# Four of six modulation parts as running sums on VectorE, placed between the delta rule's first pair of heads and the retention

## The chip, the cores and the metric

The kernel runs on 1 core of one Trainium2 chip. The metric is the device time of one execution in microseconds (us). The whole program is one launch: a first transformer block (a retention and a gated delta rule side by side, then a mixture of experts) and a second one.

## What is computed

Only the modulation matters here. A conditioning vector goes through silu and a 1024 by 6144 matrix, a bias is added, and the 6144 results are cut into six vectors of 1024: shift, scale and gate of the mixer, shift, scale and gate of the feed-forward part. The first two of the six are also wanted for a second vector, that of the context.

```python
def _modulation(cvec, w, b, n):
    m = jax.nn.silu(cvec) @ w[:, : n * D_MODEL] + b[: n * D_MODEL]
    return jnp.split(m, n, axis=-1)
...
        sh1, sc1, g1, sh2, sc2, g2 = [m[:, None, :] for m in _modulation(c, w_mod[i], b_mod[i], 6)]
        cm = _modulation(c_ctx, w_mod[i], b_mod[i], 2 if last else 6)
```

The second block does the same with its own matrix (`w_mod_2`), where the context needs its first two vectors too.

## The kernel before, in words

**Parts.** Each of the two matrices is worked in three parts of 2048 columns (`bk` 0, 1, 2), six parts in all. `mod_part` (from L298) does one part: for each of eight row tiles `k` it loads 128 by 2048 weights (1 MB) over SP's queue, one tile ahead, and issues four TensorE matmuls (L309), one for each 512 columns, which sum over `k` in one PSUM bank. Then ScalarE copies the bank (`brow`, L313), TensorE transposes it, and VectorE adds the bias into `mcol` (L321). The stationary operand `cm` holds both vectors in two of its 32 columns, so that one pass gives both.

**Order of the work.** The order is written by hand with Python generators. The dense products of the projections (`feat3`, which are the L253 matmuls: float32 as two rounded halves, three products) are the backbone; after every six matmuls of 512 columns `tick` gives each generator in `chains` one turn, that is, runs it to its next `yield`. One turn's instructions so stand in the engines' queues between those six matmuls and the next. A scheduler may still shift instructions a little. Each engine then runs its own queue in order.

**The stretch.** `phase_a` does: part 0 of the first matrix (needed at once); then, for each of two pairs of delta-rule heads (p = 0, 1), `gdn_feats` (keys, values and queries of the pair, six projections), eight `gate_spill` projections and two `out_gate` projections; then the same for two pairs of retention heads, shorter; then `mix_out`. Beside these run the chains. `gdn_chain` of a pair inverts the pair's triangular matrices (`gdn_inverse`) once the keys are there, on VectorE: a transpose into `Bk` (L914), 31 steps of a product and a subtraction (`it`, L918, and `T`, L919), and two transposes back (`Tc`, L923, and `Uc`, L924). TensorE's first matmuls on the result are L948. After that the pair's scan over six chunks runs as a chain beside the next pair's projections. `later_mods` is a chain too: it is started before the first pair, and makes parts 1 and 2 of the first matrix and all three of the second, each row tile followed by two turns (`pause` 2).

**Weights.** The tiles of the projection weights (1 MB each) and of the modulation weights take turns in one pool of four buffers (`wp`), in the order in which they are asked for, all over SP's queue (L176). A projection tile is split into halves by ScalarE (`wsh`, L211) and GpSimd (`wsl`, L212), which frees its buffer.

Of the kernel before, what the change touches and what calls it, by code (L numbers as in the profile page):

```python
# [16 lines left out]
OP = mybir.AluOpType  # L17
# [4 lines left out]
P = 128  # L22
D = 1024
ND = 8
# [74 lines left out]
AHEAD, EARLY = 2, (2, 2, 3, 3)  # L99
W1, W2, W4, W5 = 5.5, 1.8, 6.0, 3.0  # L100
TAPS = 16

LOADS2, ORDER2 = 12, "vvvvbb"

# [14 lines left out]
class K:  # L119
# [180 lines left out]
    def mod_part(self, w, b, cm, mcol, bk, pause):  # L300
# [19 lines left out]
        for r in range(2):  # L320
            nc.vector.tensor_add(dst[:, :, :, r], pt.rearrange("p j (g q) -> p g j q", g=4)[:, :, :, r],  # L321
                                 self.bcol[:, 48 * b + 16 * bk:48 * b + 16 * bk + 16].rearrange("p (g j) -> p g j", g=4))

    def bcast_row(self, cols, name):

        nc = self.nc
        dst = self.u(D, name=name)
        for h in range(2):
            ps = self.ps(4, P)
            self.transposes(ps, [cols[:, 4 * h + k:4 * h + k + 1].to_broadcast([P, P]) for k in range(4)])  # L330
            nc.scalar.copy(dst[:, h * 512:(h + 1) * 512], ps.rearrange("p a b -> p (a b)"))
        return dst
# [77 lines left out]
    def phase_a(self):  # L410
        nc, a, cp = self.nc, self.a, self.cp
        self.setup()
        self.w_in1()
        xt = [self.u(D, name="xt") for _ in range(4)]
        ct = [self.u(D, name="ct") for _ in range(2)]
        for t in range(2):
            nc.scalar.dma_start(ct[t], a["ctx"][t * P:(t + 1) * P])
        for t in range(4):
            nc.scalar.dma_start(xt[t], a["x"][t * P:(t + 1) * P])
        cm = self.silu_cols(R_C, "1")  # L420
        mcol = self.mcol = cp.tile([P, 48, 2], F32, name="mcol1")
        hc, hx = [], []
        self.start(self.rows_T(ct, hc, "hc", 5), self.rows_T(xt, hx, "hx", 4))
        for i, _ in enumerate(self.mod_part("w_mod", 0, cm, mcol, 0, 3)):
            if i in (10, 11):
                self.w_fetch(i - 10)
            if i in (22, 23):
                for _ in self.w_split(i - 22, 0):
                    pass
            self.tick()  # L430
        self.drain()
        gm = self.col[:, R_GMIX:R_GMIX + 8]
        Ax = self.mod_cols(gm, mcol, 1, 0, "x1")
        Ac = self.mod_cols(gm, mcol, 1, 1, "c1")
        self.hx = self.split_T(hx, 2, Ax, mcol[:, 0:8, 0], "hx", nc.vector)
        self.hc = self.split_T(hc, 4, Ac, mcol[:, 0:8, 1], "hc", nc.gpsimd)
        del hx, hc
        self.ghalf = cp.tile([P, 8], F32, name="ghalf")
        nc.vector.tensor_scalar(self.ghalf, self.col[:, R_RGN:R_RGN + 8], 0.5, None, op0=OP.mult)
        self.yT = [[None, None], [None, None]]  # L440
        self.gsp = self.dp.tile([16, P, NX], F32, name="gsp")
        self.start(self.later_mods(cm))
        self.gates_ab()
        gs = [SimpleNamespace(p=p, k=0, v=0, q=0, z=[]) for p in range(2)]
        for g in gs:
            self.gdn_feats(g)
            self.start(self.gdn_chain(g))
            for i in range(8):
                self.gate_spill(8 * g.p + i)
            self.out_gate(g)  # L450
        rs = [SimpleNamespace(p=p, z=[]) for p in range(2)]
        for r in rs:
            self.ret_feats(r)
            self.start(self.ret_chain(r))
            self.out_gate(r)
        self.mT = self.mix_out()

    def later_mods(self, cm):
        nc = self.nc
        yield from self.ret_consts()  # L460
        for bk in (1, 2):
            yield from self.mod_part("w_mod", 0, cm, self.mcol, bk, 2)
        cm2 = self.silu_cols(R_C2, "2")
        mcol = self.mcol2 = self.cp.tile([P, 48, 2], F32, name="mcol2")
        for bk in range(3):
            yield from self.mod_part("w_mod_2", 1, cm2, mcol, bk, 2)

    def w_stream(self, name, tiles, ahead, depth=1):

# [1397 lines left out]
    def phase_c(self):  # L1867
# [3 lines left out]
        ys, taps = self.conv_mixer(h)  # L1871
        qkv, rest = self.attn_proj(h, itertools.islice(taps, TAPS))
        self.attention(qkv, rest, itertools.chain(taps, self.conv_tail(ys)))
# [529 lines left out]
```

## Time and profile before

| what | us |
|---|---|
| median of 3 runs (2783.3 to 2787.47) | 2784.44 |
| the profiled execution | 2782.33 |
| its span in the trace | 2780.3 |
| TensorE (PE) busy | 2487.4 |
| VectorE (DVE) busy | 1061.3 |

The profiled execution took 2.0 us more than its span (start and end outside the trace) and 2.1 us less than the median. The table of stretches below cuts the time from 57 us on: 57 to 232 is the first pair of heads (p = 0) up to its output gate, 232 to 423 the second pair (p = 1), 423 to 625 the two pairs of the retention. Of the modulation, the five later parts lie between 57 and 300 us.

### The profile page before, as it was taken

How to read it: one execution, taken by the hardware profiler on the slowest of the kernel's cores; microseconds unless marked ns; L12 is line 12 of the kernel's file. 1: busy time of each engine (PE TensorE's matmuls, PEld its weight loads, DVE VectorE, ACT ScalarE, POOL GpSimd, SP SyncE). 2: the span in 40 equal slices, each digit the busy share in tenths (PEclk: the TensorE clock that was granted, in tenths of full speed). 3: DMA queues.
4: the chain of work that ended last, by engine and by line, in shares of the span. 5: the costliest groups of instructions: out<-in, count | busy, mean ns of one | idle time of the engine just before them, and what ended most of it. 6: DMA issues, size and time to landing. Idle time of an engine off the chain costs nothing.

```text
span 2780.3 us, 35001 instructions
## 1 busy us (share of the span) xinstructions
PE 2487.4 (89%) x13409; PEld 1371.2 (49%) x13409; DVE 1061.3 (38%) x2677; ACT 515.1 (19%) x1088; POOL 516.7 (19%) x390
## 2 busy tenths in 40 slices
PE   6999989999799998988797979979999899998996
PEld 3767869887545543433344867423333333332332
DVE  3573763464733532222224796321211212112122
ACT  4443532223211111000112225200000000000001
POOL 3152243334212222222233520000000000000000
PEclk8999999999899999999898989989999999999999
DMA  7676321234479999999998122359999999999996
GB/s 268 220 270 221 96 88 38 70 118 152 160 248 322 344 347 331 357 350 322 330 333 248 47 97 81 144 248 415 426 427 427 427 427 426 427 427 427 427 427 292
DMA packets 160155, 782.14 MB, mean 281 GB/s; under 512 B 20787, under 2 KB 66035, under 8 KB 121075
## 3 DMA queue, kind: packets, MB, share of 16 engines
q1 hardware_dynamic: 132080, 716.74, 66.0%
q0 software_dynamic: 16288, 37.79, 5.7%
q10 hardware_dynamic: 11618, 25.35, 2.5%
q8 instruction: 107, 1.75, 0.3%
q14 instruction: 62, 0.50, 0.1%
HBM read 752.73 MB, written 33.23 MB: 283 GB/s over the span
## 4 chain that ended last, share of the span: by engine, by line
PE 64%; DMA 18%; DVE 13%; issue 2%; ACT 2%; POOL 0%; SPq 0%; DVEq 0%; ACTq 0%; POOLq 0%
PE ps L253 16%; PE ps L2269 13%; PE ps L2288 8%; DMA wu<-in_w_expert 7%; PE ps L228 5%; DMA w<-in_w_expert 5%; PE ps L1642 5%; DMA wd<-in_w_expert 4%; PE ps L224 3%; DVE cy L1905 3%; PE ps L2217 2%; PE ps L2300 2%; PE ps L309 2%; PE ps L1639 1%; DMA acb<-ey,sidx 1%
## 5 line engine op out<-in xcount | busy, mean ns | idle before, releaser
L2269 PE MATMUL ps<-w,xT 128*64 128x512 f32 x2048 | 444.3, 593 | 6.5 <-DMA w<-in_w_expert 4.9
L2269 PEld LDWEIGHTS ps<-w,xT 128*64 128x64 f32 x2048 | 147.1, 137 | 301.2 <-issue 278.2
L2288 PE MATMUL ps<-w,hT 128*64 128x512 f32 x1024 | 233.0, 614 | 18.7 <-ACT hT L2280 18.7
L2324 POOL TENSOR_TENSOR fin<-fin,norm_final_g 128x512 f32<-128x512 f32 x2 | 2.6, 1312 | 1111.3 <-ACT fin L2317 1111.3
L212 POOL TENSOR_TENSOR wsl<-w,wsh 128x1024 fp32r<-128x1024 f32 x60 | 154.0, 2576 | 260.3 <-ACT wsh L211 213.2
L2275 DVE TENSOR_TENSOR hid<-hid,ps 128x512 f32<-128x512 f32 x32 | 22.0, 688 | 404.2 <-PE ps L2269 404.2
L1642 PE MATMUL ps<-w,xT 128*128 128x512 f32 (+6 forms) x320 | 154.4, 627 | 19.9 <-DMA w<-in_w_expert 11.8
L224 PE MATMUL ps<-wd,ehT 128*128 128x512 f32 (+6 forms) x320 | 151.6, 618 | 16.3 <-DVE eh L1653 12.7
L2288 PEld LDWEIGHTS ps<-w,hT 128*64 128x64 f32 x1024 | 74.3, 142 | 169.0 <-issue 143.9
L1642 PE MATMUL ps<-wu,xT 128*128 128x512 f32 (+6 forms) x320 | 145.8, 595 | 0.0
L1608 POOL DMA_INDIRECT xg<-h2d,sidx x65 | 67.2, 1033 | 326.5 <-PE ps L1672 169.6
L1663 DVE COPY ehT<-ps 128x256 f32<-128x256 f32 (+6 forms) x69 | 22.8, 331 | 272.4 <-PE ps L228 272.4
L2293 DVE TENSOR_TENSOR y<-ps,G 128x512 f32<-128x512 f32 x16 | 11.1, 692 | 272.2 <-PE ps L2288 272.2
L2274 ACT ACTIVATE hid<-ps 128x512 f32<-128x512 f32 x32 | 19.1, 597 | 516.4 <-PE ps L2269 516.4
L1652 ACT ACTIVATE eh<-ps 128x256 f32<-128x256 f32 (+6 forms) x69 | 23.3, 338 | 492.2 <-PE ps L1642 315.1
L1905 DVE SCALAR_TENSOR_TENSOR cy<-cv,cw,cy 128x512 f32<-128x512 f32 x120 | 109.3, 972 | 0.3
L1642 PEld LDWEIGHTS ps<-w,xT 128*128 128x128 f32 (+6 forms) x320 | 54.2, 173 | 110.9 <-issue 101.7
L224 PEld LDWEIGHTS ps<-wd,ehT 128*128 128x128 f32 (+6 forms) x320 | 51.8, 172 | 86.2 <-issue 59.7
L253 PE MATMUL ps<-hxh,wsh 128*128 128x512 f32 x296 | 88.1, 426 | 5.6 <-ACT wsh L211 3.1
L2303 DVE TENSOR_TENSOR xr<-xr,ps 128x512 f32<-128x512 f32 x128 | 78.2, 681 | 19.4 <-PE ps L2300 19.4
L1642 PEld LDWEIGHTS ps<-wu,xT 128*128 128x128 f32 (+6 forms) x320 | 50.2, 164 | 71.1 <-issue 68.1
L228 PE MATMUL ps<-cst,xg 64*128 64x64 f32 (+7 forms) x584 | 65.0, 247 | 20.2 <-DVE xg L2220 12.7
(643 smaller groups left out, 4169.2 us busy)
## 6 DMA issues: line engine op xcount, KB each, us to landing
w<-in_w_expert SPq DMA_DIRECT2D x191, 2048.0 KB, 17.1
w<-in_w_expert SPq DMA_DIRECT2D x64, 1024.0 KB, 15.6
wu<-in_w_expert SPq DMA_DIRECT2D x128, 512.0 KB, 16.2
wd<-in_w_expert SPq DMA_DIRECT2D x128, 512.0 KB, 14.3
w<-in_w_mod SPq DMA_DIRECT2D x48, 1024.0 KB, 5.8
w<-in_w_in SPq DMA_DIRECT2D x34, 1024.0 KB, 5.7
wa<-in_w_in SPq DMA_DIRECT2D x9, 512.0 KB, 9.9
gsp<-gsp POOLq DMA_DIRECT2D x16, 256.0 KB, 3.6
```

Of the source, the lines that this page charges most:

```text
L212: (lo or self.nc.vector).tensor_sub(low, x, hi.bitcast(F32))
L224: self.nc.tensor.matmul(ps, l, r, start=(i == 0), stop=(i == n - 1))
L228: self.nc.tensor.transpose(ps[:, i], s, self.ident[:parts, :parts])
L253: self.nc.tensor.matmul(ps, l, r, start=(i == 0), stop=(i == n - 1))
L309: nc.tensor.matmul(ps[32 * g:32 * g + 32, :], cm[:, k, :], wt[:, g * 512:(g + 1) * 512], start=(k == 0), stop=(k == ND - 1), tile_position ...
L1608: self.nc.gpsimd.indirect_dma_start(out=self.xg[b % 4][:c], out_offset=None, in_=self.h2d, in_offset=bass.IndirectOffsetOnAxis(ap=idx[:c], ...
L1642: nc.tensor.matmul(ps[:m], x, w[k], start=first, stop=last)
L1905: nc.vector.scalar_tensor_tensor(y[:, j], vs[j][:, k:k + NX], tap, y[:, j], op0=OP.mult, op1=OP.add)
L2217: nc.tensor.matmul(px[64 * j:64 * j + 64], Gt[:, t], hs[t][:, 512 * j:512 * j + 512], start=(t == 0), stop=(t == 3), tile_position=(0, 64 ...
L2269: nc.tensor.matmul(pgu[gi][c][64 * j:64 * j + 64], xT[:, k], w[2 * j + c], start=(k == 0), stop=(k == ND - 1), tile_position=(0, 64 * j))
L2288: nc.tensor.matmul(py[64 * j:64 * j + 64], hT[fc][:, ff, 64 * fj:64 * fj + 64], w[2 * r + j], start=(ft == 0), stop=(ft == 15), tile_posit ...
L2303: nc.vector.tensor_add(xh, xh, ps)
```

## The change

`later_mods` no longer starts before the first pair but after it, and `ret_consts`, which stood at its head, starts alone in the old place. Parts 1 and 2 of both matrices are made by a new function, `mod_row`: VectorE multiplies each row tile by the silu of its rows (a value for each partition) and adds it to a running sum, two instructions of 128 by 1024 for each tile (the first tile's without the addition), each followed by one turn. At the end of a part four TensorE matmuls with a matrix of ones add the 128 partitions up. Part 0 of the second matrix, which needs both vectors, stays as it was and comes last.

```diff
+    def mod_row(self, w, b, cm, mcol, bk, pause):
...
+        acc, nxt = [self.u(D, name="macc") for _ in range(2)], load(0)
+        for k in range(ND):
+            wt, nxt = nxt, load(k + 1) if k + 1 < ND else None
+            for h in range(2):
+                v = wt[:, h * D:(h + 1) * D]
+                if k == 0:
+                    nc.vector.tensor_scalar(acc[h], v, cm[:, k, 0:1], None, op0=OP.mult)
+                else:
+                    nc.vector.scalar_tensor_tensor(acc[h], v, cm[:, k, 0:1], acc[h], op0=OP.mult, op1=OP.add)
+                for _ in range(pause):
+                    yield
+        ps, brow = self.ps(), self.u(512, name="brow")
+        for g in range(4):
+            nc.tensor.matmul(ps[32 * g:32 * g + 32], self.ones[:, 0:32], acc[g // 2][:, g % 2 * 512:g % 2 * 512 + 512],
+                             start=True, stop=True, tile_position=(0, 32 * g))
...
     def phase_a(self):
...
-        self.start(self.later_mods(cm))
+        self.start(self.ret_consts())
...
             self.out_gate(g)
+            if g.p == 0:
+                self.start(self.later_mods(cm))
...
     def later_mods(self, cm):
-        nc = self.nc
-        yield from self.ret_consts()
         for bk in (1, 2):
-            yield from self.mod_part("w_mod", 0, cm, self.mcol, bk, 2)
+            yield from self.mod_row("w_mod", 0, cm, self.mcol, bk, MODS)
         cm2 = self.silu_cols(R_C2, "2")
         mcol = self.mcol2 = self.cp.tile([P, 48, 2], F32, name="mcol2")
-        for bk in range(3):
-            yield from self.mod_part("w_mod_2", 1, cm2, mcol, bk, 2)
+        for bk in (1, 2):
+            yield from self.mod_row("w_mod_2", 1, cm2, mcol, bk, MODS)
+        yield from self.mod_part("w_mod_2", 1, cm2, mcol, 0, 2)
```

`MODS` is 1. In the changed kernel line numbers are higher: L309 becomes L310, L253 L254, L918 L951, L923 L956 and L948 L981; the new sums are L336 (first tile) and L338, the ones matmuls L343.

The places where the order moves follow. First TensorE, among the gate projections of the first pair (`ps_...<-hxl,wsh` and so on), before:

```order
L253 MATMUL ps_1475<-hxl_339,wsh_1445 128x512 x2
L309 MATMUL ps_1418<-w_1521,cm_295_1409 32x512
L699 MATMUL ps_1550<-qT_1348,gkT_452 128x128 x4
L253 MATMUL ps_1564<-hxh_317,wsh_1539 128x512 x2
L253 MATMUL ps_1564<-hxh_324,wsh_1539 128x512 x2
L253 MATMUL ps_1564<-hxh_331,wsh_1539 128x512 x2
L309 MATMUL ps_1418<-w_1521,cm_295_1409 32x512 x3
L253 MATMUL ps_1564<-hxh_338,wsh_1539 128x512 x2
```

and the same place now:

```order
L254 MATMUL ps_1341<-hxl_339,wsh_1311 128x512 x2
L229 MATMUL ps_1364<-cst,qn_1238 128x128 x4
L229 MATMUL ps_1381<-cst,qw_1362 128x128 x4
L732 MATMUL ps_1404<-qT_1239,gkT_452 128x128 x4
L254 MATMUL ps_1418<-hxh_317,wsh_1393 128x512 x2
L254 MATMUL ps_1418<-hxh_324,wsh_1393 128x512 x2
```

The modulation's matmuls are gone from the first pair; 32 groups of four become 4 groups of four in the whole program, and the eight groups of the part that stays move into the retention.

Second VectorE, at the start of the second pair's inverse, before:

```order
L918 TENSOR_TENSOR it_3495<-Bk_3470,T_3405 128x112
L919 TENSOR_TENSOR T_3405<-T_3405,it_3495 128x28x4
L918 TENSOR_TENSOR it_3511<-Bk_3470,T_3405 128x135
L919 TENSOR_TENSOR T_3405<-T_3405,it_3511 128x27x5
L918 TENSOR_TENSOR it_3514<-Bk_3470,T_3405 128x156
```

and now:

```order
L951 TENSOR_TENSOR it_3306<-Bk_3265,T_3194 128x112
L338 SCALAR_TENSOR_TENSOR macc_3294<-w_3298,cm_740_3286,macc_3294 128x1024
L338 SCALAR_TENSOR_TENSOR macc_3295<-w_3298,cm_740_3286,macc_3295 128x1024
L952 TENSOR_TENSOR T_3194<-T_3194,it_3306 128x28x4
L742 TENSOR_TENSOR qw_3386<-qn_3050,eg 128x512
L742 TENSOR_TENSOR qw_3408<-qn_3169,eg 128x512
L736 TENSOR_TENSOR QE_2481<-QE_2481,ps_3362 128x512
L736 TENSOR_TENSOR QE_2482<-QE_2482,ps_3362 128x512
L951 TENSOR_TENSOR it_3323<-Bk_3265,T_3194 128x135
L338 SCALAR_TENSOR_TENSOR macc_3294<-w_3335,cm_740_3286,macc_3294 128x1024
L338 SCALAR_TENSOR_TENSOR macc_3295<-w_3335,cm_740_3286,macc_3295 128x1024
L952 TENSOR_TENSOR T_3194<-T_3194,it_3323 128x27x5
```

Of the 64 new instructions 16 stand between the first pair's output gate and the second pair's first keys, 16 more ahead of the second pair's inverse, 16 inside it, 16 behind it.

Third SP's queue of loads during that inverse, now (what each load waits for is in brackets; Pool and DVE stand for the reader that frees the buffer; `in_w_mod` is here the second matrix):

```order
L177 DMA w_3298<-in_w_mod 128x2048 [waits DMAHW0_49,DVE_49]
L177 DMA w_3335<-in_w_mod 128x2048 [waits DMAHW2_49,DVE_49]
L177 DMA w_3383<-in_w_mod 128x2048 [waits DMAHW7_49,Pool_49]
L177 DMA w_3422<-in_w_mod 128x2048 [waits DMAHW3_49,DVE_49]
L177 DMA w_3458<-in_w_in 128x8x256 [waits DMAHW4_49,DVE_49]
L177 DMA w_3467<-in_w_mod 128x2048 [waits DMAHW5_49,DVE_49]
```

Before, the same place held projection tiles alone, which wait for Pool; now five of six loads there wait for VectorE's sums to free a buffer, and a projection tile stands behind them.

## Rows read from the trace of the kernel before

**Rows 1.** Windows view: us, busy us of each engine, PEclk, DMA share, GB/s.

```profile
57.00:145.00 88.00, 84.53 (x509) 59.80 (x510) 42.71 (x128) 38.08 (x94) 30.89 (x26) 0.98 0.57 200
145.00:201.20 56.20, 56.20 (x308) 36.44 (x306) 49.41 (x117) 20.61 (x46) 22.72 (x26) 1.00 0.79 273
201.20:232.00 30.80, 30.80 (x428) 20.21 (x424) 5.90 (x16) 14.02 (x34) 14.46 (x21) 1.00 0.75 266
232.00:289.00 57.00, 57.00 (x368) 40.97 (x365) 21.74 (x66) 15.34 (x37) 13.06 (x10) 1.00 0.59 204
289.00:354.30 65.30, 61.71 (x409) 54.42 (x408) 56.28 (x165) 36.16 (x111) 20.96 (x21) 1.00 0.23 73
354.30:391.20 36.90, 25.67 (x123) 20.50 (x121) 34.55 (x71) 8.80 (x13) 12.90 (x13) 0.96 0.26 86
391.20:423.00 31.80, 31.76 (x417) 24.85 (x418) 8.93 (x18) 15.75 (x35) 18.77 (x22) 0.94 0.27 84
423.00:625.00 202.00, 194.52 (x1417) 182.75 (x1415) 97.97 (x325) 47.58 (x103) 67.04 (x45) 0.99 0.24 78
```

**Rows 2.** Windows view of L309 alone: us, PE and PEld busy, PEclk, DMA.

```profile
57.00:145.00 88.00, 18.66 (x112) 2.93 (x112) 0.98 0.57 200
145.00:201.20 56.20, 12.49 (x88) 1.96 (x88) 1.00 0.79 273
201.20:232.00 30.80, 5.19 (x44) 0.79 (x40) 1.00 0.75 266
232.00:289.00 57.00, 11.87 (x76) 1.68 (x72) 1.00 0.59 204
289.00:354.30 65.30, 1.06 (x8) 0.16 (x8) 1.00 0.23 73
```

**Rows 3.** Timeline of PE: start us, us, instruction, idle before in brackets.

```profile
200.20 1.07 PE L309 MATMUL ps<-w,cm 128*32 128x512 f32 x8
201.20 0.31 PE L948 MATMUL ps<-Tc,Lc 32*32 32x32 f32 x8
...
391.24 1.07 PE L948 MATMUL ps<-Tc,Lc 32*32 32x32 f32 x32 [8.13 <-DVE Tc L923]
```

**Rows 4.** Timeline of VectorE: the inverse's transposes in both pairs of heads.

```profile
195.05 2.30 DVE L923 STREAM_TRANSPOSE Tc<-T 128x1024 f32<-128x1024 f32 x1
...
354.30 1.99 DVE L914 STREAM_TRANSPOSE Bk<-Ad 128x1024 f32<-128x1024 f32 x1
...
389.21 1.97 DVE L923 STREAM_TRANSPOSE Tc<-T 128x1024 f32<-128x1024 f32 x1
```

**Rows 5.** Source view of three VectorE lines: durations in ns, min/median/max.

```profile
L1404 DVE TENSOR_SCALAR xt<-xt,rs x4: 748/749/753, 30.0 to 32.0; 128x1024 f32<-128x1024 f32 x4
...
L1468 DVE SCALAR_TENSOR_TENSOR mix<-xr,rs,Ar x2: 1274/1276/1277, 707.0 to 708.2; 128x1024 f32<-128x1024 f32 x2
...
L1338 DVE SCALAR_TENSOR_TENSOR moe<-moe,rs,G x4: 1279/1285/3370, 1505.8 to 1514.7; 128x1024 f32<-128x1024 f32 x4
```

**Rows 6.** Source view of L872, whose second tensor lies in PSUM.

```profile
L872 DVE SCALAR_TENSOR_TENSOR gz<-gz,ps x8: 676/688/690, 231.9 to 587.0; 128x512 f32<-128x512 f32 x8
```

**Rows 7.** Timelines of VectorE and GpSimd at 368 us.

```profile
368.20 2.50 DVE L919 TENSOR_TENSOR T<-T,it 128x247 f32<-128x247 f32 x1
...
367.80 5.16 POOL L212 TENSOR_TENSOR wsl<-w,wsh 128x1024 fp32r<-128x1024 f32 x2 [0.72 <-ACT wsh L211]
```

**Rows 8.** Windows view of GpSimd's `wsl` alone.

```profile
232.00:289.00 57.00, 9.50 (x4) 1.00 0.59 204
```

**Rows 9.** DMA issues, to 900 us: count, KB each, median us to landing.

```profile
w<-in_w_mod SPq DMA_DIRECT2D x48, 1024.0 KB, 5.8
```

**Rows 10.** Waits of PE in the retention: us in total, times, longest us.

```profile
PE ps L228 <- DVE go L782: 4.1, 1, 4.1
```

More of the change, by code (lines that the diff above doesn't have):

```diff
@@ L101 @@
 TAPS = 16
+MODS = 1
 LOADS2, ORDER2 = 12, "vvvvbb"
@@ L322, in mod_part @@
                                  self.bcol[:, 48 * b + 16 * bk:48 * b + 16 * bk + 16].rearrange("p (g j) -> p g j", g=4))
+    def mod_row(self, w, b, cm, mcol, bk, pause):
+        nc = self.nc
+        load = lambda k: self.wload(self.a[w][k * P:(k + 1) * P, bk * 2048:(bk + 1) * 2048])
+        acc, nxt = [self.u(D, name="macc") for _ in range(2)], load(0)
[13 more added lines that the diff above has]
+                             start=True, stop=True, tile_position=(0, 32 * g))
+        yield
+        nc.scalar.copy(brow, ps)
+        yield
+        yield
+        pt = self.ps(4, P)
+        self.transposes(pt, [brow[:, j * P:(j + 1) * P] for j in range(4)])
+        yield
+        dst = mcol.rearrange("p (b g j) r -> p b g j r", b=3, g=4)[:, bk, :, :, 0]
+        nc.vector.tensor_add(dst, pt.rearrange("p j (g q) -> p g j q", g=4)[:, :, :, 0],
+                             self.bcol[:, 48 * b + 16 * bk:48 * b + 16 * bk + 16].rearrange("p (g j) -> p g j", g=4))
     def bcast_row(self, cols, name):
```

## The prediction

> **What bounds the kernel now.** I read the stretches first, all engines in one table, then the modulation's matmuls in the same stretches, then the timelines at the two inverses. In [rows 1] TensorE is busy in all but a few us from 57 to 289; nothing else limits the first pair of heads. In [rows 2] the modulation has 36.34 us of that busy time from 57 to 232 (18.66 + 12.49 + 5.19), 11.87 from 232 to 289 and 1.06 after: each us of it is a us of the path. From 289 on it is otherwise: VectorE is busy 56.28 of 65.3 us, then 34.55 of 36.9 [rows 1], and at 391.24 TensorE has stood idle 8.13 us for `Tc`, the inverse's result, though no modulation is left there [rows 3]. So the second pair already ends on VectorE, and its inverse, from `Bk` at 354.30 to `Tc` at 389.21 [rows 4], is one serial chain. The change takes work from an engine that is the bound in the first pair and gives more of it to an engine that is the bound in the second.
>
> **First pair, 57 to 232.** Nothing is added; 36.34 us of matmuls go [rows 2]. Up to 145 I let all 18.66 go, since VectorE is busy only 42.71 of 88 us there [rows 1]. From 145 to the first L948 at 201.20, TensorE would need 56.20 - 12.49 = 43.7 us. But L948 needs `Tc`, which is ready at 195.05 + 2.30 = 197.35, 52.3 us after 145 [rows 4]. VectorE is idle 56.2 - 49.41 = 6.8 us in the stretch [rows 1]; I let half of it, 3.4, be squeezed out, which makes 48.9 us. TensorE arrives 5.2 us too early and waits for VectorE, as the second pair does now. L948 so comes 18.66 + 56.2 - 48.9 = 26.0 us earlier. Behind it 5.19 us go whole, since the same steps in the second pair (391.2 to 423) keep TensorE busy without any modulation [rows 1]. Sum **-31.2**; with nothing squeezed out -27.8, with no wait at all -36.3.
>
> **One running sum.** The nearest row is exact in form: scalar_tensor_tensor, 128x1024, float32, both tensors in SBUF, 1.276 us (L1468); the first tile's tensor_scalar takes 0.75 us (L1404) [rows 5]. A part has 14 of the one and 2 of the other, 14 x 1.276 + 2 x 0.75 = 19.4 us. The same form has also taken 3.370 us (L1338 [rows 5]), 2.1 more than its median. In the inverse a subtraction took 2.50 us while GpSimd ran two `wsl` splits [rows 7]. So I charge 2.1 us for each `wsl` that a busier VectorE now meets.
>
> [...]
>
> **Second pair up to its inverse's end, 232 to 391.2.** Three parts, 48 sums, stand here in VectorE's queue.
> - 232 to 289 holds one part. TensorE's need falls to 57.0 - 11.87 = 45.1. VectorE's is 21.74 + 19.4 = 41.1, and 8.4 for the four `wsl` there [rows 8], so 49.5. The scan's steps go back and forth between the engines, so I add 4 of idle: 53.5, **-3.5**. Low end -11.9 (TensorE alone counts), high end 0.
> - 289 to 354.3 holds one part: 56.28 + 19.4 = 75.7, 2.1 for one more `wsl`, and 3.5 idle where 9.0 was (the sums fill part of the gaps): 81.3, **+16.0**. Low end 75.7 - 65.3 = +10.4, high end +23 (all 9.0 of idle kept, two `wsl`).
> - 354.3 to 391.2, the inverse, holds one part. VectorE's gaps there are only 2.4 us, between dependent steps [rows 1], and L948 already waits: **+19.4**. Low end +17, high end +25 (one weight tile late by the 5.8 us that a load takes to land [rows 9]).
>
> Together **+31.9**, from +15.5 to +48. The ones matmuls and transposes of the first two parts are hidden here, because TensorE waits for VectorE; if that cover goes they cost 1.07 us each for the matmuls, one group of L309's price [rows 3].
>
> **Behind the inverse, 391.2 to 423.** The fourth part's 19.4 us fit beside VectorE's 8.93 in 31.8 us, but they stand in its queue ahead of the inverse's small copies from PSUM, for which TensorE waits a few us later, and TensorE has no slack (31.76 of 31.8 busy [rows 1]). The long waits before also lower the granted clock, 0.94 here behind the 8.13 us wait. I take **+3**, between 0 and +8.
>
> **Retention, 423 to 625.** The part that stays on TensorE moves here: eight groups at 1.07 us [rows 3], and two groups of ones, **+10.7**. TensorE is busy 194.52 of 202 us, and its longest wait, 4.1 us for VectorE's `go` [rows 10], ends a chain that the new matmuls don't shorten. Low end +3, if all 7.5 us of idle took some of it.
>
> **SP's queue.** The loads are as many as before, 1 MB each. In the second pair they now wait for buffers that VectorE frees, with projection tiles behind them. A load takes 5.8 us to land and two sums take at least 2.55, but up to three tiles stand ready, so I cost it at nothing beside the high end above; the cover is TensorE's wait for VectorE. GpSimd's queue changes only in that its splits meet more VectorE work; its own time is off the path. The shorter first pair shifts ScalarE's copies, at no cost.
>
> **Sum.** -31.2 + 31.9 + 3 + 10.7 = +14.4 us. Against the profiled execution's 2782.33 that gives 2796.7. The median of the runs is 2.1 higher, so I predict **2799 us**. Later stages follow unchanged and are only shifted. The ends alone would give -18 to +39, about 2767 to 2823; they don't all fall on one side together.
>
> **Rivals.**
> - **Faster: VectorE has room until the inverse.** Then the 32 sums ahead of the inverse vanish in its gaps (57.0 - 21.74 = 35.3 us of idle in the first stretch and 9.0 in the second, 44 in all, against 38.8 of sums), the matmuls' 11.87 + 1.06 are won there too, and only the inverse pays: -31.2 - 12.9 + 19.4 + 10.7 = -14, that is **2770**. It decides if from 289 to 354 TensorE still sets the pace (61.71 us of busy). For it: most gaps lie before 289. Against: 56.28 + 19.4 is already above 65.3 there.
> - **No change.** First pair -36, second pair +24, +12 behind: **2784**. It needs VectorE's inverse to begin early enough in the first pair that nothing waits for it, and the sums to fill every gap. For it: both are ends of my terms. Against: the 5.2 us wait above comes out of rows.
> - **Slower still: loads set VectorE's pace.** In the inverse the buffers come free only as VectorE and the splits finish, each load then takes 5.8 us [rows 9], and VectorE, waiting in order, holds up the inverse. If four of the eight tiles there come late by that time, +23 more: **2822**. It decides where a tile's load is issued less than 5.8 us before its first sum. For it: SP's order above. Against: loads are issued up to three tiles ahead.
> - That the change doesn't do what it says can be left out: the order shows 4 groups of ones in place of 32 groups.
>
> **How the numbers follow.** Forecast 0.56, faster rival 0.16, no change 0.16, loads 0.12. The forecast's own range is 2788 to 2812. The 8 in 10 range leaves out most of the faster rival and the far end of the loads: **2778 to 2819**. About 0.2% (5.6 us) is what a measurement of this kernel can tell from no change. Faster by more than that: 0.16, the faster rival. Within it: 0.17, the no-change case and a sliver of the forecast. Slower: 0.67, the rest of the forecast and the loads.
>
> **What the new profile would show.** L310 has a third of L309's matmuls. The sums (L338) number 56, 1.28 us at the least, 1.35 to 1.5 on average. TensorE waits some 5 us for `Tc` in the first pair, at about 175 us; in the second it waits at `Tc` and before it for 30 us or more in all, and that wait ends at about 392. VectorE is busy over 90% from the first output gate to there. Wrong would be: L981 reached in the second pair before 385 us (the sums had room, so the faster rival), VectorE idle inside the inverse with DMA as releaser (the loads), or sums near 2.5 us.

## The result, and the profile after

The changed kernel takes 2833.27 us (median of 4 runs, 2821.91 to 2842.54) against 2785.95 (4 runs, 2783.3 to 2789.06): 1.0169 times as long, 95% interval 1.0151 to 1.0188. It is slower by 47 us. The direction was forecast, the size (+14, range up to 2819) was not. The profiled execution took 2838.17 us, 55.8 more than that of before.

Where the 55.8 us lie is read from instructions that occur in both programs, five in the first stage and four behind it (start in us; gV,R is the first matmul of a pair's scan, gz the retention's last output gate):

| instruction | before | changed | shift | step |
|---|---|---|---|---|
| matmul gV,R, first pair | 238.64 | 227.71 | -10.9 | first pair -10.9 |
| transpose Bk, second pair | 354.30 | 359.07 | +4.8 | second pair before the inverse +15.7 |
| matmul Tc,Lc, second pair | 391.24 | 416.26 | +25.0 | inverse +20.2 |
| matmul gV,R, second pair | 423.38 | 450.16 | +26.8 | behind the inverse +1.8 |
| last gz | 587.00 | 620.85 | +33.9 | retention +7.1 |
| first block's experts, next to last ey | 1472.3 | 1500.1 | +27.8 | output projection and experts -6 |
| sum of the experts, first moe | 1498.8 | 1533.3 | +34.5 | +6.7 |
| first tap of the second block's convolution, cy | 1553.4 | 1590.5 | +37.1 | +2.6 |
| third of the convolution's four results, yc | 1714.0 | 1771.5 | +57.5 | +20.4 |

So 33.9 us come from the stretch that the change touches, and some 22 more from places 850 us and more behind it: the steps of -6 and +6.7 cancel, and what is left is the second block's. First the windows view of the changed kernel, cut at the same instructions (us, then the busy time of PE, PEld, DVE, ACT and POOL, granted clock, DMA share, GB/s):

```profile
57.00:194.70 137.70, 111.90 (x602) 95.53 (x602) 91.00 (x231) 56.61 (x136) 53.70 (x50) 0.92 0.18 58
194.70:222.40 27.70, 27.64 (x384) 21.25 (x384) 7.57 (x17) 13.28 (x32) 15.61 (x20) 0.90 0.28 96
222.40:359.10 136.70, 112.24 (x679) 98.06 (x679) 114.30 (x249) 50.44 (x147) 35.69 (x30) 0.91 0.45 156
359.10:416.20 57.10, 33.47 (x160) 24.80 (x158) 54.47 (x103) 9.82 (x16) 12.88 (x11) 0.90 0.57 207
416.20:449.80 33.60, 33.54 (x421) 25.89 (x422) 26.43 (x31) 16.35 (x36) 21.31 (x25) 0.91 0.60 216
449.80:658.90 209.10, 205.43 (x1497) 184.44 (x1495) 107.97 (x337) 49.45 (x106) 69.62 (x45) 1.00 0.40 134
```

In [rows 1] TensorE had no more than 3.5 us of idle up to the first pair's inverse. Now it is idle 25.8 of 137.7 us there, while VectorE is busy 91.0. Its waits, from the view of waits from 57 to 222 us (total, times, longest):

```profile
PE ps L254 <- POOL hcl L420: 6.3, 1, 6.3
PE ps L229 <- DVE gK L687: 5.6, 2, 4.1
PE ps L600 <- DVE la L595: 4.2, 1, 4.2
PE ps L229 <- DVE qw L742: 3.4, 1, 3.4
PE ps L981 <- DVE Tc L956: 3.4, 1, 3.4
PE ps L254 <- DVE hxl L420: 1.9, 1, 1.9
PE ps L254 <- ACT wsh L212: 1.6, 1, 1.6
PE ps L732 <- ACT qT L700: 0.9, 2, 0.7
```

They come to 27.3 us, on three engines and eight tiles. Before, all its waits from 57 to 230 us were 4.8 us, the two below and two of 0.5:

```profile
PE ps L567 <- DVE la L562: 1.9, 1, 1.9
PE ps L253 <- DVE hxl L388: 1.9, 1, 1.9
```

Only one of the new ones, `Tc`, is a wait that I had forecast. In the timeline of TensorE the two longest stand back to back, and the gap between two matmuls of the same product is plain to see:

```profile
68.45 0.64 PE L254 MATMUL ps<-hcl,wsh 128*128 128x256 f32 x4
75.36 2.08 PE L254 MATMUL ps<-hcl,wsh 128*128 128x256 f32 x8 [6.27 <-POOL hcl L420]
77.36 0.39 PE L229 MATMUL ps<-cst,abT 16*128 16x16 f32 x2
81.91 1.48 PE L600 MATMUL ps<-la,cst 128*128 128x48 f32 x6 [4.15 <-DVE la L595]
```

The granted clock, 0.98 and 1.00 in [rows 1], is 0.92 now. Behind the wait for `Tc` it is 0.50, while TensorE is busy all the time, so that what follows this idle spell is slower as well: eight matmuls that take 1.98 us at a granted 1.00 took 3.78 there (timeline of PE, then the windows view of the same two places):

```profile
194.76 1.07 PE L981 MATMUL ps<-Tc,Lc 32*32 32x32 f32 x32 [3.40 <-DVE Tc L956]
195.76 3.78 PE L254 MATMUL ps<-hxh,wsl 128*128 128x512 f32 x8
...
225.44 1.98 PE L254 MATMUL ps<-hxh,wsl 128*128 128x512 f32 x8
```

```profile
195.80:199.40 3.60, 3.60 (x11) 2.83 (x10) 0.70 (x1) 2.43 (x9) 3.48 (x4) 0.50 0.00 0
225.44:227.30 1.86, 1.86 (x10) 1.54 (x9) 1.86 (x2) 0.00 (x0) 1.15 (x1) 1.00 0.00 0
```

In the second pair VectorE is busy 54.47 of 57.10 us of the inverse. The sums there, from the windows view of L338 alone, and TensorE's wait at their end (timeline of PE):

```profile
222.40:359.10 136.70, 39.00 (x28) 0.91 0.45 156
359.10:416.20 57.10, 19.17 (x14) 0.90 0.57 207
416.20:449.80 33.60, 13.82 (x9) 0.91 0.60 216
449.80:658.90 209.10, 8.70 (x6) 1.00 0.40 134
```

```profile
416.26 0.84 PE L981 MATMUL ps<-Tc,Lc 32*32 32x32 f32 x22 [15.66 <-DVE Tc L956]
```

That answers to the 8.13 us in [rows 3]. Far behind, in the second block, stands something that no row of before had. GpSimd's `wsl` took 2.5 to 6 us beside the second block's convolution before; here one took 34.35 (source view of L213, minimum, median and maximum in ns). It ran beside 48 sums of a convolution on VectorE that follow each other without a gap (timeline of DVE), and TensorE waited for it (timeline of PE):

```profile
L213 POOL TENSOR_TENSOR wsl<-w,wsh x12: 2362/2391/34352, 1597.1 to 1712.3; 128x1024 fp32r<-128x1024 f32 x12
```

```profile
1629.44 31.89 DVE L1938 SCALAR_TENSOR_TENSOR cy<-cv,cw,cy 128x512 f32<-128x512 f32 x48
```

```profile
1663.58 3.78 PE L263 MATMUL ps<-hph,wsl 128*128 128x512 f32 x8 [23.42 <-POOL wsl L213]
```

The profiler's spans on GpSimd are rough, but TensorE's 23.42 us say the same. VectorE then waits 24.4 us for a bias table (`bt`), but that is a link of the same chain: ScalarE, which asks for the table at 1681.3, had waited for the matmuls that the split held up.

### The profile page after: what moved, and what is told of

Same layout as the page of the kernel before. It is cut to its first block, busy times and chain, and to the rows that moved or that the text cites. A ratio compares the mean times of both kernels' runs of the same rounds, so it can differ in the third digit from the quotient of the medians.

```text
span 2836.4 us, 34623 instructions
## 1 busy us (share of the span) xinstructions
PE 2473.7 (87%) x13185; PEld 1383.0 (49%) x13185; DVE 1134.5 (40%) x2737; ACT 514.9 (18%) x1088; POOL 552.9 (19%) x390
## 5 line engine op out<-in xcount | busy, mean ns | idle before, releaser
L213 POOL TENSOR_TENSOR wsl<-w,wsh 128x1024 fp32r<-128x1024 f32 x60 | 181.8, 3039 | 281.7 <-ACT wsh L212 158.4
L1675 PE MATMUL ps<-w,xT 128*128 128x512 f32 (+6 forms) x320 | 146.6, 601 | 13.8 <-DVE xT L1659 7.3
L254 PE MATMUL ps<-hxh,wsh 128*128 128x512 f32 x296 | 88.0, 432 | 13.6 <-ACT wsh L212 11.0
L1938 DVE SCALAR_TENSOR_TENSOR cy<-cv,cw,cy 128x512 f32<-128x512 f32 x120 | 96.7, 868 | 0.4
L2336 DVE TENSOR_TENSOR xr<-xr,ps 128x512 f32<-128x512 f32 x128 | 78.2, 681 | 19.4 <-PE ps L2333 19.4
L254 PE MATMUL ps<-hxh,wsl 128*128 128x512 f32 x296 | 84.8, 425 | 0.9 <-POOL wsl L213 0.9
```

The source lines that it names most:

```text
L213: (lo or self.nc.vector).tensor_sub(low, x, hi.bitcast(F32))
L254: self.nc.tensor.matmul(ps, l, r, start=(i == 0), stop=(i == n - 1))
L1675: nc.tensor.matmul(ps[:m], x, w[k], start=first, stop=last)
L1938: nc.vector.scalar_tensor_tensor(y[:, j], vs[j][:, k:k + NX], tap, y[:, j], op0=OP.mult, op1=OP.add)
L2336: nc.vector.tensor_add(xh, xh, ps)
```

## Experiments

Three theories were tried. **A**: the modulation's matmuls had filled waits of TensorE in the first pair, and the sums cost VectorE's time in the second pair. **B**, the forecast's: TensorE alone sets most of the first pair, so matmuls taken from it come back in full. **L**: a split on GpSimd is shut out while VectorE's two-input sums follow each other. The table has every run's times for the same instructions as above (profiled executions) and the median time; before ran again beside each batch, at 2783.27, 2783.61 and 2784.80 us.

| run | gV,R first pair | Tc,Lc second pair | gV,R second pair | last gz | median, us |
|---|---|---|---|---|---|
| before | 238.6 | 391.2 | 423.4 | 587.0 | 2785.95 |
| changed | 227.7 | 416.3 | 450.2 | 620.9 | 2833.27 |
| again | 226.6 | 419.3 | 453.0 | 623.7 | 2831.53 |
| move_only | 226.7 | 394.4 | 431.9 | 601.9 | 2800.78 |
| gap | 225.5 | 417.8 | 451.8 | 622.6 | 2820.81 |
| small_sums | 227.3 | 381.5 | 415.8 | 585.4 | 3498.94 |
| pace2 | 225.4 | 404.5 | 438.2 | 626.9 | 2837.77 |
| split | 235.1 | 383.5 | 416.5 | 596.8 | 2795.67 |
| slow | 236.5 | 390.3 | 423.8 | 588.8 | 2793.45 |
| sums_early | 293.9 | 446.4 | 478.5 | 642.1 | 2839.39 |
| one_part | 227.3 | 418.6 | 457.7 | 622.2 | 2825.00 |
| hc_dve | 222.7 | 416.0 | 449.6 | 620.4 | 2813.35 |
| before_gap | 238.7 | 392.7 | 425.9 | 590.7 | 2785.75 |
| hold | 230.0 | 383.7 | 416.6 | 581.3 | 2781.25 |

Again and the changed kernel are one program, and before_gap has the program of before up to the last gz; they differ by up to 4 us there. Smaller differences in this table say nothing.

**again** (no edit).

> The changed kernel once more, unaltered. In its profile one split on GpSimd (wsl, normally 2.4 us) took 34.4 us while VectorE ran 48 convolution sums of the second block without a gap, and TensorE waited 23.4 us for it. If the order of the queues decides that, a split of over 25 us stands in this profile too and the time is 2825 to 2842. If it is a matter of when the split happens to arrive, this profile may lack it, and then the span is about 2836 - 23 = 2813.

Ratio 1.0158, interval 1.0125 to 1.0191. The long split is there again, 33.80 us, and the profiled execution took 2837.28 us. The four runs are 2818.89, 2825.78, 2837.28 and 2838.43 us, those of the first measurement 2821.91 to 2842.54. So it comes with this order of the queues, but perhaps not each time: whether the shorter two lack it no trace shows.

**move_only.**

```diff
     def later_mods(self, cm):
-            yield from self.mod_row("w_mod", 0, cm, self.mcol, bk, MODS)
+            yield from self.mod_part("w_mod", 0, cm, self.mcol, bk, 2)
...
-        for bk in (1, 2):
-            yield from self.mod_row("w_mod_2", 1, cm2, mcol, bk, MODS)
-        yield from self.mod_part("w_mod_2", 1, cm2, mcol, 0, 2)
+        for bk in range(3):
+            yield from self.mod_part("w_mod_2", 1, cm2, mcol, bk, 2)
```

> Only the move: all five later parts stay matmuls on TensorE, but begin after the first pair. Theory A (the waits of the first pair had been covered by the modulation): the first pair ends as in the changed kernel, L1022's second group at 219.8 +- 2 us and not near 198; the second pair then takes five parts of some 9.9 us each on TensorE, of which its 15 us of idle before hide some: the retention ends 20 to 30 us later than in the kernel before. Theory B (my forecast's: TensorE alone sets the first pair): the first pair ends 31 us earlier, near 198, and the retention ends 0 to 10 us later than before.

Theory A. The first pair ends at 226.7, as in the changed kernel, and the group named above starts at 218.8, where B wanted 198. The retention ends 14.9 us later, less than the 20 to 30 I expected. Ratio 1.0063, interval 1.0046 to 1.0080: the move alone costs 17 us, and the sums, which were to make up for it, another 30.

**gap.**

```diff
     def conv_taps(self, i, vs, y):
+        gap = self.u(2, name="gap")
...
+            if k % 4 == 3:
+                nc.vector.tensor_copy(gap, y[:, :, 0])
             yield
```

> The changed kernel, with a copy of 128x2 on VectorE after every fourth tap of the second block's convolution, which breaks the run of 48 two-input sums into pieces of at most 12. Theory L (a split on GpSimd is shut out as long as such sums follow each other): no split takes over 12 us, TensorE's wait of 23 us for wsl is gone, and the time falls to 2805 to 2815. Rival (the long split is only a symptom; the second block waits for something else, the bias tables bt say): the time stays at 2825 to 2840.

The longest split is now 3.79 us (source view of L213), and TensorE's 23 us are gone:

```profile
L213 POOL TENSOR_TENSOR wsl<-w,wsh x12: 2382/2658/3790, 1596.7 to 1695.1; 128x1024 fp32r<-128x1024 f32 x12
```

Theory L's expectation came true, and VectorE's wait for the bias table, the rival's cause, is gone with the split. In one place a split and a copy end together: the longest split, 3.79 us, stood over two whole sums and ended at 1672.42, the copy behind these sums at 1672.45, after 2.30 us where four of the other five in this timeline took 0.15 or 0.16 (timelines of GpSimd and VectorE):

```profile
1668.63 3.79 POOL L213 TENSOR_TENSOR wsl<-w,wsh 128x1024 fp32r<-128x1024 f32 x1 [22.44 <-ACT wsh L212]
...
1670.15 2.30 DVE L1941 COPY gap<-cy 128x2 f32<-128x2 f32 x1
```

But the splits at 1639.76 and 1643.64 took 2.96 and 2.56 us inside a run of twelve sums, without a copy, and one_part and hc_dve below have no long split and no copies. Whether the copies, or only another timing of the split, spared this run the long one is not shown. The profiled execution took 2819.61 us, 17.7 less than that of again on the same chip. The medians differ by 10.7 us, and the time missed the 2805 to 2815. The ratios to before, 1.0141 (1.0124 to 1.0159) and 1.0158 (1.0125 to 1.0191), overlap, so the gain over all runs isn't settled.

**small_sums.** It leaves out 1016 of each sum's 1024 columns. The modulation is then another one, the second block's tokens go to other experts, and its time is not compared; the first stage's instructions are.

```diff
-                    nc.vector.scalar_tensor_tensor(acc[h], v, cm[:, k, 0:1], acc[h], op0=OP.mult, op1=OP.add)
+                    nc.vector.scalar_tensor_tensor(acc[h][:, 0:8], v[:, 0:8], cm[:, k, 0:1], acc[h][:, 0:8], op0=OP.mult, op1=OP.add)
```

> The changed kernel with the running sums cut to 8 of 1024 columns (their loads, count, turns and the ones matmuls stay; the modulation made from them is left out in effect). It prices VectorE's time in the sums. Theory A with my second-pair terms (sums cost VectorE 20 us in the inverse and 14 before it): the first pair ends as in the changed kernel (near 219.8), the inverse's first matmuls L981 come at 375 to 383 in place of 416, and the retention ends 25 to 40 us earlier than in the changed kernel. Rival (loads or turns, not the sums, hold the second pair up): L981 stays beyond 400.

```profile
381.51 0.84 PE L981 MATMUL ps<-Tc,Lc 32*32 32x32 f32 x22 [1.50 <-DVE Tc L956]
```

The sums' own time is the cost: 416.3 - 381.5 = 34.8 us up to here, with loads, turns and ones matmuls as before. The run shows a second thing. From the first pair's gV,R to this matmul it takes 154.2 us, where before took 152.6 with 11.7 us of modulation matmuls in it. So the matmuls had cost no more there than the short sums and the ones matmuls that replace them. A cleaner price comes from run split, whose second pair has no modulation at all (windows view from its gV,R to its Bk, then to its Tc,Lc): 148.4 us, 4.2 less than before.

```profile
235.10:347.00 111.90, 101.51 (x655) 91.03 (x653) 79.41 (x224) 47.82 (x144) 31.20 (x30) 0.97 0.15 46
347.00:383.50 36.50, 24.97 (x118) 20.01 (x117) 34.34 (x71) 8.44 (x13) 11.78 (x12) 0.94 0.22 77
```

With the matmuls gone from both pairs and the sums nearly free, Tc,Lc comes 9.7 us earlier than before, all of it gained in the first pair (11.3). So taking the matmuls off TensorE is worth some 10 to 16 us in the two pairs (estimated from 9.7, and from 11.3 + 4.2), however well their work is hidden elsewhere.

**pace2** (`MODS = 2`).

> The changed kernel with two turns after each running sum, so that half as many of the sums stand in the second pair and the other half in the retention. So far: with the sums cut short L981 comes at 381.5, with full sums at 416.3. If the sums cost VectorE's time in proportion (theory A), L981 comes at 396 to 404. If sums are nearly free in the retention, where VectorE is busy 98 of 202 us, the retention's last output gate comes at 598 to 606; if they cost as much there, at 615 to 622. Time with the long split 2805 to 2825, without it 2795 to 2805.

Tc,Lc at 404.5, at the edge of what was expected: 28 of the 56 long sums are behind it. The last gz, 626.9, is later than either theory had it: from Tc,Lc to there it takes 222.4 us, against 203.9 in small_sums. The sums cost there too, 18.5 us, though VectorE is busy only 98 of 202 us in [rows 1]. This run has no long split (at most 4.99 us) and still takes 2837.77 us, well above what I expected; only 40 of its 54 us stand at the last gz, and the rest stays open.

**split.** Two generators in place of one:

```diff
+    def first_mods(self, cm):
+        for bk in (1, 2):
+            yield from self.mod_part("w_mod", 0, cm, self.mcol, bk, 2)
+        self.cm2 = self.silu_cols(R_C2, "2")
+        self.mcol2 = self.cp.tile([P, 48, 2], F32, name="mcol2")
+        yield from self.mod_part("w_mod_2", 1, self.cm2, self.mcol2, 0, 2)
+
+    def later_mods(self):
+        for bk in (1, 2):
+            yield from self.mod_row("w_mod_2", 1, self.cm2, self.mcol2, bk, 2)
...
-        self.start(self.ret_consts())
+        self.start(self.ret_consts(), self.first_mods(cm))
...
-            if g.p == 0:
+            if g.p == 1:
```

> A candidate: parts 1 and 2 of the first matrix and part 0 of the second as matmuls on TensorE from the first pair on, as before the change; parts 1 and 2 of the second matrix as running sums, started after the second pair's output gate, two turns apart. Theory A: the first pair's waits cover most of the three parts (30 us of matmuls), the second pair has no modulation, and the sums fall into VectorE's gaps of the retention: retention's last output gate 580 to 590 against 587.0 before, time 2775 to 2790. Rival (a sum of 1.3 us stands in the way of every reply that TensorE waits for in the retention, or splits collide): 595 to 610, time 2790 to 2810.

The rival. Up to Tc,Lc it gains 7.7 us, and the retention gives back more: from the second gV,R to the last gz 180.3 us against 163.6 before, 16.7 for two parts. TensorE's longest waits there are for VectorE, whose queue holds the sums (view of waits from 383 us on, behind the inverse's own):

```profile
PE ps L1155 <- DVE rS L1139: 3.3, 1, 3.3
PE ps L254 <- DVE vp L849: 2.8, 1, 2.8
PE ps L873 <- DVE vt L862: 2.8, 2, 2.3
```

Ratio 1.0060, interval 1.0038 to 1.0083.

**slow.**

```diff
-            yield from self.mod_part("w_mod", 0, cm, self.mcol, bk, 2)
+            yield from self.mod_part("w_mod", 0, cm, self.mcol, bk, 3)
...
-            yield from self.mod_part("w_mod_2", 1, cm2, mcol, bk, 2)
+            yield from self.mod_part("w_mod_2", 1, cm2, mcol, bk, 3)
```

> The kernel before with three turns in place of two after each row tile of the modulation: all parts stay on TensorE from the first pair on, and a third of what stood in the first pair moves to the second. Theory A (the first pair paid 12 us for 36 us of matmuls, the second pair pays nothing for 13 us): the first pair ends 2 to 6 us earlier than before, the second pair's L948 comes 0 to 5 us earlier, time 2777 to 2783. Rival (the second pair has no more room than 13 us): L948 as before or up to 8 us later, time 2783 to 2792.

The first pair ends 2.1 us earlier, Tc,Lc 0.9, and the last gz comes 1.8 later: no change in this stage. Yet the time is 1.0032 times that of before (1.0016 to 1.0048), because the sum of the experts starts 12.0 us later than before (1510.8 against 1498.8), 10.2 of it arising behind the last gz, and the last yc 15.7 us later.

**sums_early.**

```diff
-        self.start(self.ret_consts())
+        self.start(self.ret_consts(), self.later_mods(cm))
...
-            if g.p == 0:
-                self.start(self.later_mods(cm))
```

> The changed kernel's running sums at the old place: the same later parts, but begun before the first pair. Theory A says that the first pair too ends on VectorE and on replies to TensorE, so the sums there cost as they do in the second pair: first pair's L979 (first matmuls on the inverse) at 215 to 240 against 194.8 in the changed kernel, second pair then without any cost of the modulation (its length from there to its own L979 about 190 us), retention's last output gate 600 to 625. Rival (VectorE idle for half of the first pair has room): L979 at 195 to 203 and the last output gate at 575 to 590, faster than before.

Worse than either: Tc,Lc of the first pair at 249.1, 54 us behind the changed kernel's 194.8. Up to there VectorE does 45 sums, which take it 61.5 us, so most of their time is on the path, in a stretch in which VectorE had been idle for a third of the time. Part of the 54 us is TensorE's clock, granted at 0.81 there against 0.92. TensorE's waits from 57 to 250 us:

```profile
PE ps L229 <- DVE gK L685: 19.1, 2, 11.4
PE ps L979 <- DVE Tc L954: 15.0, 1, 15.0
PE ps L229 <- DVE it L949: 8.1, 1, 8.1
```

`gK` had been 5.6 us. The same small replies, later.

**one_part.**

```diff
-        self.start(self.ret_consts())
+        self.start(self.ret_consts(), self.mod_part("w_mod", 0, cm, self.mcol, 1, 2))
...
-        for bk in (1, 2):
-            yield from self.mod_row("w_mod", 0, cm, self.mcol, bk, MODS)
+        yield from self.mod_row("w_mod", 0, cm, self.mcol, 2, MODS)
```

> The changed kernel with one part (part 1 of the first matrix, 9.9 us of matmuls) back on TensorE from the start of the first pair, and three parts as running sums after it. Cover theory: the matmuls fill TensorE's first waits, so the first pair ends (first L854) 0 to 3 us later than in the changed kernel's 226 to 228. TensorE-bound theory: 8 to 10 us later, 235 to 238. The three parts of sums keep their pace of one a turn and still fill the second pair up to the end of its inverse, so L981 comes at 410 to 420 as before; the retention has less behind it and ends 0 to 8 us earlier than the changed kernel's 621.

The first pair ends at 227.3 with 9.9 us of matmuls put back, the same as without: they are free. All of them run before 78 us, where they take the place of the wait for `hcl`, which is gone; what matmuls cost later in the pair this run doesn't tell (hold does). Tc,Lc at 418.6 is as expected; the retention does not end earlier, though no sums are left behind Tc,Lc. From there to the last gz it takes 203.6 us, the changed kernel 204.6: its 15 sums behind Tc,Lc had cost about 1 us.

**hc_dve.**

```diff
-        self.hc = self.split_T(hc, 4, Ac, mcol[:, 0:8, 1], "hc", nc.gpsimd)
+        self.hc = self.split_T(hc, 4, Ac, mcol[:, 0:8, 1], "hc", nc.vector)
```

> The changed kernel with the context's low halves (hcl) made by VectorE and not by GpSimd, which takes away TensorE's first long wait of the first pair, 6.3 us. If that wait is a cost of its own, everything behind it in the first pair comes 4 to 6 us earlier, first L854 at 221 to 224. If the waits are links of one chain over VectorE and ScalarE (the next one, la, takes its place), it moves by less than 2 us, 225 to 229, or later because VectorE has more to do.

The first pair ends at 222.7, some 4 us earlier than in again: most of that wait of 6.3 us was a cost of its own. It is lost by Tc,Lc, 416.0 against 416.3, where VectorE sets the time. The long split is absent here (5.96 us at most) and the time is 2813.35 us.

**before_gap** (the edit of gap, on the kernel before).

> The kernel before, with the copies between the convolution's taps that run gap had. In the kernel before no split took over 6 us, so shutting out costs little there: time within 4 us of 2783, no split over 4 us. If the copies themselves were what helped run gap (by another order of VectorE's queue), this one would be faster by 8 us or more too.

Ratio 1.0003, interval 0.9992 to 1.0014: the copies as such help nothing.

**hold.**

```diff
     def later_mods(self, cm):
+        for i, _ in enumerate(self.all_mods(cm)):
+            if i == HOLD_AT:
+                for _ in range(HOLD):
+                    yield
+            yield
+
+    def all_mods(self, cm):
```

with `HOLD_AT, HOLD = 64, 24`.

> A candidate: the kernel before with a pause of 24 turns in the modulation, placed where the first pair's TensorE work behind its inverse (L959 and what follows) has no waits to fill; the eight or so row tiles concerned move into the second pair, which paid nothing for its 13 us of matmuls. Cover theory: the first pair ends 3 to 6 us earlier (first gV,R group at 233 to 236 against 238.6), the second pair's first matmuls on its inverse 0 to 5 us earlier (386 to 391), the time 2778 to 2784 where nothing behind moves. Rival: as with three turns a tile, the last tiles reach the second pair's tail and the gain is gone: retention's last output gate at 587 to 592.

In this stage it does what the cover theory says, and better. The modulation's matmuls behind the first inverse go down to 1.18 us (windows view of its line, L311) and 14.29 stand in the second pair:

```profile
198.10:230.00 31.90, 1.18 (x12) 0.16 (x8) 1.00 0.50 158
230.00:383.70 153.70, 14.29 (x112) 2.51 (x112) 0.98 0.43 148
```

The first pair ends 8.6 us earlier than before, Tc,Lc comes 7.5 earlier and the last gz 5.7. The time is 2781.25 us over 10 runs against 2784.80: ratio 0.9987, interval 0.9972 to 1.0002, so not told apart from no change. In its trace the 5.7 us are gone again behind the experts: their sum starts 1.5 us later than before. For the argument the run shows most of all what the first pair pays: with 31.09 of the 37.6 us of matmuls ahead of its inverse (windows view of L311) it ends 2.3 to 4.6 us later than the six runs that have none there and are otherwise the same up to it (225.4 to 227.7).

## Why the prediction was wrong

- **First pair, "-31.2": -10.9. This step failed,** and in its part ahead of the inverse. L948 was to come 26.0 us earlier; the same matmul comes 6.4 earlier (201.20 to 194.76). The 5.19 us behind it, which were to go whole, brought 4.5. "Up to 145 I let all 18.66 go, since VectorE is busy only 42.71 of 88 us there" took a busy share for slack, and "each us of it is a us of the path" took TensorE's busy time for need. TensorE was busy throughout because the modulation filled its waits for single replies (27.3 us now). Eight runs with no modulation in the first pair, or one part of it, end it between 222.7 and 227.7, one_part shows 9.9 us of it there to be free, and hold shows 31.09 us ahead of the inverse to cost 5 us at most. The sum had one such reply, `Tc`, at 5.2 us (3.40 measured), and the other seven at nothing. The 1.9 us for `la` before a matmul of before was a row that could have warned: a wait that shows through while the filler is there.
- **Second pair to its inverse's end, "+31.9": +35.9.** The inverse's +19.4 is +20.2, from 14 sums that took 19.17 us and two short ones: right in kind and size. Before it I forecast -3.5 + 16.0 = +12.5, measured +15.7, and that this is close is in part luck. I charged 10.5 us (8.4 + 2.1) for splits that meet a busier VectorE; the 28 sums there took 39.00 us, only 3.3 more than 28 times 1.276. And I left VectorE 7.5 us idle (4 + 3.5), where it is idle 22.4 of 136.70 us, most of it behind results of TensorE. The two errors hide each other. What the sums cost from the first pair's gV,R to Tc,Lc is 34.4 us (188.6 - 154.2, by small_sums).
- **Price of a sum.** The row's 1.276 us held: L338's median is 1.278, its mean 1.47 (source view of L338, in ns, and view of lines). That is 1.86 times L872's 0.688 us for half as many columns with the second tensor in PSUM [rows 6].

```profile
L338 DVE SCALAR_TENSOR_TENSOR macc<-w,cm,macc x56: 1267/1278/3405, 227.7 to 460.2; 128x1024 f32<-128x1024 f32 x56
```

- **Behind the inverse, "+3": +1.8. Retention, "+10.7": +7.1**, with 8.52 us of the remaining part's matmuls in it. Both lie inside their ranges.
- **"Later stages follow unchanged and are only shifted": +22 in the profiled execution, +13 by the medians (47.3 - 33.9). This step failed too.** Output projection and experts take 6 us less, and the sum of the experts gives them back, since VectorE waits 27.7 us for the experts' results and not 21.0. SP asks for these results in another order (before in turns of three, three, one and one, now four and four), but the order is not the cause: hc_dve, which asks as before does, waits 28.0 us, and pace2, which asks as the changed kernel does, 24.5. What sets this wait stays open (views of waits of before, changed, hc_dve and pace2):

```profile
DVE moe L1312 <- DMA mob<-acb: 21.0, 1, 21.0
...
DVE moe L1345 <- DMA mob<-acb: 27.7, 1, 27.7
...
DVE moe L1345 <- DMA mob<-acb: 28.0, 1, 28.0
...
DVE moe L1345 <- DMA mob<-acb: 24.5, 1, 24.5
```

  The 22 us that are left lie in the second block and go with the long split. From the first moe to the last yc the two traces that have it take 238.9 us (changed) and 235.1 (again); before takes 215.9, and gap, hc_dve and one_part, which lack it, take 219.0, 214.8 and 217.3. The forecast had nothing for it.
- **The rivals.** "Loads set VectorE's pace" gave the nearest time, 2822, for a reason that didn't hold: VectorE's sums waited 4.6 us for loads in all, six times. "Faster: VectorE has room" is refuted by small_sums and, in stretches with more room, by sums_early and split, and so is "No change", which needed the sums to fill every gap.
- **The signs named in advance** came as said in the second pair (the wait for Tc ends at 416 where I said about 392, late by the first pair's missing 20 us and the second pair's 4), and the wait for `Tc` in the first pair is there; the seven others beside it were the sign that the step was wrong. VectorE was to be busy over 90% from the first output gate to the second `Tc`; it is 87% (114.30 + 54.47 of 193.8 us).

## What to carry to other kernels

An engine that is busy all the time may be so because filler work stands in its waits; what the filler costs is found by taking it out (or, as here, by shortening it to a few columns), not by adding up its busy time. Work moved to a half-idle engine that answers another engine's requests costs by how many replies it delays: one part of the modulation cost some 3 us of the path as matmuls in the first pair (11 us for 3.8 parts), and 8 to 12 as sums (16.7 for two in the retention, 34.8 for three in the second pair), though the changed kernel's last sums, behind the second inverse, cost about 1 us. Stages far behind an edit need not stay as they were: here, 850 us and more behind it, they added 22 us in the trace, so keep a part of the range for them.

## What the runs showed of the hardware

A split on GpSimd, two SBUF inputs and normally 2.4 us, took 34.35 us while VectorE ran 48 sums with two SBUF inputs back to back, each of them at 0.66 us. The ten sums from 1619.83 us on, with no split beside them, came at 0.67 (6.71 us), so the 48 were not slowed. The split ended at 1663.52, 2.2 us behind the last of them.

In the traces of before and of the changed kernel three more splits beside this convolution stood over three or more whole sums: 4.77 us from 1586.18 and 5.96 us from 1631.84 in before, 6.51 us from 1609.81 in the changed one. Each ended 2.3 us after VectorE had begun an instruction on PSUM (at 1588.61, 1635.52 and 1613.99), and the sum that follows that instruction took 2.2 to 2.3 us in place of 0.74. In gap it was the copy at 1670.15 that began 2.27 us ahead of the split's end. The other twelve splits beside the convolution in before took 2.53 to 2.91 us, and beside each of them a sum took 2.29 to 2.89 us.

What decides whether the split or the sum takes longer is not shown. In the kernel before, the split at 1597.12 us started 0.08 us after the convolution's one-input instruction and took 2.65 us, while the sum behind that instruction took 2.88; in the changed kernel the split at 1629.17 started 0.12 us after the same instruction and took 34.35 us, while the sum behind it took 0.75 (timelines of GpSimd and VectorE).

```profile
1597.12 2.65 POOL L212 TENSOR_TENSOR wsl<-w,wsh 128x1024 fp32r<-128x1024 f32 x1 [0.55 <-ACT wsh L211]
```
